# Shorter look-aheads in a pipelined segment mean: indices 7 rows ahead, boundaries closed by three, ids summed 4 ahead

**Chip and metric.** One core of one Trainium2 chip. The metric is device time in microseconds (us) of one execution; medians and ranges are over all executions of a set. A few executions run over 1.5% longer than the fastest of the same kernel; they are called slow, and ratios leave them out. Before: 189.45 us (188.91 to 191.78).

## The reference

```python
n, num_segments = 10_000_000, 10000
data = np.random.randn(n).astype(np.float32)
segment_ids = np.sort(np.random.randint(0, num_segments, n))      # int64, sorted

np.add.at(sums, segment_ids, data)
np.add.at(counts, segment_ids, 1)
return sums / np.maximum(counts, 1)
```

## The kernel before

Each of 128 partitions owns 78,125 numbers, cut into 90 rows of 875. As the ids are sorted and a segment holds some 1,000 numbers, a row has at most about one boundary. Per row the kernel must find where it lies and split the row's sum there. It reads every 175th id (probes), computes from them which window of 175 ids holds the boundary, gathers that window, and sums it; the sum tells the exact place.

The names used below: **first look** (probes to gather indices, six rows at once, VectorE; its last step issues six gathers on GpSimd), **id sum** (`add_ids`, ScalarE), **closing** (`second_look`, VectorE: id sums to boundaries), **total** (ScalarE) and **split** (VectorE) of the row's data. The writer of the kernel fixes every engine's program order: `put(r, steps)` appends steps to what VectorE does after the split of row r, and steps put on one row run in the order in which they were put.

```python
X_PIECE = 15; PIECE = 2; X_DATA = 26; X_LOOK = 9; RING = 18; HALVES = 66
def x_sum(r):
    return 6 if r < HALVES else 5                 # rows by which ids are summed ahead
...
def second_look(a, b):                            # a closing
    ... out=KK[:, a:b], in0=YY[:, a:b], scalar=float(S // K), in1=GS[:, a:b] ...
def total(r):  nc.scalar.activation(out=junk_a, in_=d, func=ACT.Copy, accum_out=T[:, r:r+1])
def split(r):  nc.vector.scalar_tensor_tensor(in0=iota, scalar=KK[:, r:r+1], in1=d,
                   op0=ALU.is_lt, op1=ALU.mult, accum_out=A[:, r:r+1], ...)
...
for a, b in zip(bounds[1:], bounds[2:]):          # groups of six rows, 6, 12, 18, ...
    if a < HALVES:
        put(a - 1, second_look(a, b))
    else:
        put(a - 1, second_look(a, a + 3))
        put(a + 2, second_look(a + 3, b))
for g in range(HEAD, NG):                         # HEAD = 3
    if g < NG - 1:
        put(max(bounds[g] - X_LOOK, 0), first_look(g), 5)
...
for r in range(-X_PIECE - X_DATA, NR):
    while pnext < NR and pnext <= r + X_PIECE + pnext // bounds[NG - 1] + X_DATA:
        load_probes(...)                          # SyncE, two rows a piece
    while nt < NT and 2 * nt <= r + X_DATA:
        load_data(nt)                             # SyncE, two rows a tile
    while r >= -1 and gs < NR and gs <= r + x_sum(gs):
        add_ids(gs)
    if r >= 0:
        total(r); split(r)
        for f in after[r]: f()
```

(Shortened: counters, the first pieces and the steps before row 0 are left out.)

Of the kernel before, what the change touches and what calls it, by code (L numbers as in the profile page):

```python
# [22 lines left out]
NR = 90  # L23
# [4 lines left out]
NX = NR + E  # L28
FAR = float(1 << 18)
GROUPS = [6] * 15  # L30
X_PIECE = 15
PIECE = 2
X_DATA = 26
X_LOOK = 9
RING = 18
HALVES = 66
NO = 79
SHIFT = 6
ND = 2 * SHIFT + 1
# [79 lines left out]
def kernel(  # L119
# [21 lines left out]

    ctx.enter_context(tc.manual_schedule())

    def x_sum(r):
        return 6 if r < HALVES else 5


    pr = cpool.tile([P, NR + 1, K], I64, name="pr")
# [7 lines left out]
    bounds = [0]  # L156
# [3 lines left out]
    def load_probes(r0, r1):  # L160
        a = 0 if r0 == 0 else K * r0 + 1
        b = min(K * r1 + 1, NPR)
        nc.sync.dma_start(out=pr_flat[:, a:b], in_=ids_p[:, a * S : (b - 1) * S + 1 : S])
# [3 lines left out]
    def load_data(t):  # L167
        d = dpool.tile([P, 2 * L], FP32, name="data_t")
        a, b = 2 * t * L, min(2 * (t + 1) * L, D)
        c = b if t < NT - 1 else a + L  # L170
        nc.sync.dma_start(out=d[:, 0 : c - a], in_=data_p[:, a:c])
        if c < b:
            nc.sync.dma_start(out=d[:, c - a : b - a], in_=data_p[:, c:b])
        tiles[t] = d
# [9 lines left out]
    def view(ap, dims):  # L184
        return bass.AP(ap.tensor, ap.offset, [list(ap.ap[0])] + dims)
# [71 lines left out]
    def first_look(g):  # L257

        a, b = bounds[g], bounds[g + 1]
        n = b - a  # L260
        far = fpool.tile([P, n], FP32, name="far", bufs=3)
        last = b == NR
        v = nc.vector

        def s1():
            if last:
                m = NR * K + 1 - NPR
                v.tensor_copy(
                    out=pr_flat.bitcast(I32)[:, 2 * NPR : 2 * (NPR + m)].rearrange("p (a b) -> p a b", b=2),
                    in_=view(snt32[:, 0:1], [[0, m], [1, 2]]),  # L270
                )
            v.tensor_reduce(out=SG[:, a:b], in_=pr32[:, a:b, 0 : 2 * K : 2], axis=AX.X, op=ALU.add)  # L272

        def s2():
            v.scalar_tensor_tensor(  # L275
                out=ST[:, a:b], in0=VI[:, a + 1 : b + 1], scalar=float(K), in1=SG[:, a:b],
                op0=ALU.mult, op1=ALU.subtract,
            )

        def s3():  # L280
            v.tensor_scalar(out=far, in0=ST[:, a:b], scalar1=0.0, scalar2=FAR, op0=ALU.is_equal, op1=ALU.mult)  # L281

        def s4():
            v.tensor_add(out=ST[:, a:b], in0=ST[:, a:b], in1=far)  # L284

        def s5():
            for c, d, w in [(a, b - 1, S), (b - 1, b, TAIL)] if last else [(a, b, S)]:
                v.scalar_tensor_tensor(  # L288
                    out=IDX[:, c:d], in0=ST[:, c:d], scalar=float(w), in1=wb[:, c:d], op0=ALU.mult, op1=ALU.add
                )  # L290
            v.scalar_tensor_tensor(  # L291
                out=YY[:, a:b], in0=ST[:, a:b], scalar=float(K + 1), in1=SG[:, a:b], op0=ALU.mult, op1=ALU.add
            )
            if last:
                v.tensor_scalar(
                    out=tl, in0=ST[:, NR - 1 : NR], scalar1=-1.0, scalar2=float(TAIL - S),
                    op0=ALU.add, op1=ALU.mult,
                )
            gather(g)

        return [s1, s2, s3, s4, s5]

    def gather(g):
        for r in range(bounds[g], bounds[g + 1]):
            nc.gpsimd.indirect_dma_start(  # L305
                out=GT[:, r % RING, :],
                out_offset=None,
                in_=ids2d[:],
                in_offset=bass.IndirectOffsetOnAxis(ap=IDX[:, r : r + 1], axis=0),
                bounds_check=N - W,  # L310
                oob_is_err=False,
            )

    def add_ids(r):
        nc.scalar.activation(  # L315
            out=junk_a[:, 0:W], in_=gt32[:, r % RING, 0 : 2 * W : 2], func=ACT.Copy,
            accum_out=GS[:, r : r + 1],
        )

    def second_look(a, b):  # L320
        def s1():
            nc.vector.scalar_tensor_tensor(  # L322
                out=KK[:, a:b], in0=YY[:, a:b], scalar=float(S // K), in1=GS[:, a:b],
                op0=ALU.mult, op1=ALU.subtract,
            )
            if b == NR:
                nc.vector.tensor_add(out=KK[:, NR - 1 : NR], in0=KK[:, NR - 1 : NR], in1=tl)

        return [s1]

    def total(r):
        n = min(L, D - r * L)
        d = tiles[r // 2][:, (r % 2) * L : (r % 2) * L + n]
        t = T[:, r : r + 1]
        nc.scalar.activation(out=junk_a[:, 0:n], in_=d, func=ACT.Copy, accum_out=t)  # L335
# [152 lines left out]
    def check_frame():  # L488

        return [  # L490
            lambda: v.tensor_sub(out=jb[:, 0:1], in0=base1, in1=pin),
            lambda: v.scalar_tensor_tensor(
                out=bad[:, NC + 1 : NC + 2], in0=base1, scalar=float(NT1), in1=vx, op0=ALU.add, op1=ALU.is_gt
            ),
            lambda: v.tensor_sub(out=jb[:, 1:2], in0=V[:, R2 : R2 + 1], in1=V[:, NR : NR + 1]),
            lambda: v.tensor_scalar(
                out=bad[:, NC + 2 : NC + 3], in0=delta, scalar1=0.0, scalar2=None, op0=ALU.is_lt
            ),
            lambda: v.scalar_tensor_tensor(
                out=bad[:, NC : NC + 1], in0=pc, scalar=0.0, in1=jb[:, 0:1], op0=ALU.is_equal, op1=ALU.mult  # L500
            ),
            lambda: v.tensor_scalar(
                out=bad[:, NC + 3 : NC + 4], in0=delta, scalar1=float(ND - 1), scalar2=None, op0=ALU.is_gt
            ),
            lambda: v.scalar_tensor_tensor(
                out=bad[:, NC + 4 : NC + 5], in0=jb[:, 1:2], scalar=plast[:, 0:1], in1=pone,
                op0=ALU.add, op1=ALU.is_lt,
            ),
        ]
# [159 lines left out]
    def place(c0, c1, t, outs):  # L669
        def s1():  # L670
            n = c1 - c0
            nc.vector.tensor_tensor(
                out=shf[:, c0:c1, 0:ND], in0=view(t[:, c0 : c0 + 1], [[1, n], [1, ND]]),
                in1=view(dm[:, 0:1], [[0, n], [1, ND]]), op=ALU.mult,
            )

        def s2():
            for a, b, d, o in outs:
                nc.vector.tensor_reduce(out=o, in_=shf[:, a:b, 0:d], axis=AX.X, op=ALU.add)

        return [s1, s2]
# [86 lines left out]
    NG = len(GROUPS)  # L768
# [8 lines left out]
    def put(r, steps, every=1):  # L777
        for i, f in enumerate(steps):
            after[r + i // every].append(f)
# [4 lines left out]
    for a, b in zip(bounds[1:], bounds[2:]):  # L784
        if a < HALVES:
            put(a - 1, second_look(a, b))
# [2 lines left out]
            put(a + 2, second_look(a + 3, b))  # L789
    for g in range(HEAD, NG):  # L790
        if g < NG - 1:
            put(max(bounds[g] - X_LOOK, 0), first_look(g), 5)

    def mixed(p, q):
        out = []
# [22 lines left out]
    put(59, counts(Q1, R1), 2)  # L818
    put(R1 - 1, mixed(sums(Q1, R1), select(H1, M1)) + table(H1, M1, tab), 2)
    put(64, place(0, T1, tab, [(0, C1, ND + 1, OUT[:, 0:C1]), (C1, T1, ND + 1, xa[:, 0 : T1 - C1, RM - R1])]))  # L820
    look = bounds[NG - 1] - X_LOOK - 2
    put(46, check_frame(), 2)
    put(66, check_windows())
    put(68, pick(nc.vector, pa[:, :, 0 : RM - R1], C1, CA - C1, R1, RM))
# [23 lines left out]
    pnext = 0  # L848
    nt = 0
    gs = 0  # L850
    for r in range(-X_PIECE - X_DATA, NR):
        while pnext < NR and pnext <= r + X_PIECE + pnext // bounds[NG - 1] + X_DATA:
            n = GROUPS[0] if pnext == 0 else PIECE
            load_probes(pnext, pnext + n)
            if pnext == 0:
                load_data(0)
                nt = 1
            pnext += n
        while nt < NT and 2 * nt <= r + X_DATA:
            load_data(nt)  # L860
            nt += 1
        if r == -X_DATA:
            nc.scalar.dma_start(
                out=snt[0 : P - 1, :],
                in_=segment_ids[D : N].rearrange("(p d) -> p d", d=D)[:, 0:1],
            )
        if r == -1:
            for f in after[r][: 5 * HEAD]:
                f()
        while r >= -1 and gs < NR and gs <= r + x_sum(gs):  # L870
            add_ids(gs)
            gs += 1
        if r == -1:
            for f in after[r][5 * HEAD :]:
                f()
        if r >= 0:
            total(r)
            split(r)
            for f in after[r]:
                f()  # L880
# [31 lines left out]
```

## Time and profile before

| | before |
|---|---|
| median | 189.45 us |
| span of the profiled run | 186.4 us |
| VectorE (DVE) busy | 140.8 us, 76% |
| ScalarE (ACT) busy | 136.6 us, 73% |
| 90 gathers | 14.0 MB, 23.5% of the DMA engines' span |
| data and probes | 40.5 MB, 73.8% |

No engine is busy all the time; only the DMA is, from 5 to 172 us. The lines that carry this stand in the prediction.

### The profile page before, as it was taken

To read this page: it belongs to the slowest core of one execution; us is meant where nothing else is said; L and a number is where in the kernel's file an instruction comes from. 1 tells how busy PE (TensorE), PEld (TensorE's weight loads), DVE (VectorE), ACT (ScalarE), POOL (GpSimd) and SP (SyncE) were. 2 spreads that over 40 slices of the span, in tenths; PEclk is the share of its full clock that TensorE was granted. 3 is DMA by queue.
4 is the path that set the end of the run, shared out by engine and by line. 5 is a ranking of instruction groups with operands and counts; after the bars stand their busy time and mean duration, and the time that the engine had idled before them with its cause. 6 is when DMAs were issued, how large, how long until landed. Compare 5 with 4: busy or idle time off the path is not lost.

```text
span 186.4 us, 1479 instructions
## 1 busy us (share of the span) xinstructions
PE 1.6 (1%) x6; PEld 1.4 (1%) x6; DVE 140.8 (76%) x438; ACT 136.6 (73%) x362; POOL 99.9 (54%) x119
## 2 busy tenths in 40 slices
PE   0000000000002000000000000000000000010000
PEld 0000000000001000000000000000000000010000
DVE  6321397979197796858879997686899989999881
ACT  8010599967999497895959949599886786989940
POOL 5687775076734828266471664727347287883000
DMA  6999999999999999999999999999998999999000
GB/s 28 178 178 340 331 325 328 306 341 330 316 330 319 338 333 305 326 335 332 314 310 335 318 328 317 329 344 307 326 246 246 343 405 406 405 406 391 15 0 12
DMA packets 70613, 54.63 MB, mean 293 GB/s; under 512 B 60464, under 2 KB 61032, under 8 KB 70599
## 3 DMA queue, kind: packets, MB, share of 16 engines
q1 hardware_dynamic: 64667, 40.50, 73.8%
q0 software_dynamic: 5760, 14.01, 23.5%
q14 instruction: 14, 0.11, 0.2%
q10 hardware_dynamic: 172, 0.00, 0.1%
HBM read 56.59 MB, written 0.04 MB: 304 GB/s over the span
## 4 chain that ended last, share of the span: by engine, by line
DMA 33%; issue 32%; ACT 14%; POOL 13%; DVE 4%; POOLq 1%; ACTq 0%
DMA GT<-in_segment_ids_dram,IDX 23%; POOL GT L305 12%; DMA data_t<-in_data_dram 10%; ACT junk_a L335 9%; ACT junk_a L315 5%; POOLq L305 1%; DVE jj L236 0%; POOL i_i L198 0%; DVE junk_v L340 0%; DVE most L745 0%; DVE add L737 0%; POOL pb L703 0%; DVE sel L648 0%; DVE most L751 0%; POOL KL L689 0%
## 5 line engine op out<-in xcount | busy, mean ns | idle before, releaser
L305 POOL DMA_INDIRECT GT<-in_segment_ids_dram,IDX x90 | 90.9, 1010 | 66.9 <-ACT junk_a L315 33.5
L340 DVE SCALAR_TENSOR_TENSOR junk_v<-iota,q,data_t 128x875 bf16<-128x875 f32 x90 | 100.6, 1118 | 8.0 <-DMA data_t<-in_data_dram 6.7
L335 ACT ACTIVATE junk_a<-data_t 128x875 bf16<-128x875 f32 x90 | 83.6, 929 | 3.7 <-DMA data_t<-in_data_dram 0.7
L315 ACT ACTIVATE junk_a<-GT 128x175 bf16<-128x175 int32 x90 | 32.4, 360 | 38.1 <-DMA GT<-in_segment_ids_dram,IDX 35.9
L322 DVE SCALAR_TENSOR_TENSOR q<-YY,GS 128x6 f32<-128x6 f32 (+1 forms) x19 | 3.3, 171 | 21.7 <-ACT junk_a L315 21.7
L315 ACT ACTIVATION_READ_ACCUMULATOR junk_a<-GT 128x1 f32 x90 | 16.8, 187 | 0.0
L335 ACT ACTIVATION_READ_ACCUMULATOR junk_a<-data_t 128x1 f32 x90 | 16.8, 186 | 0.0
L340 DVE DVE_READ_ACCUMULATOR junk_v<-iota,q,data_t 128x1 f32 x90 | 7.4, 83 | 0.0
L272 DVE TENSOR_REDUCE SG<-pr 128x6 f32<-128x30 int32 x15 | 2.7, 180 | 5.7 <-DMA snt<-in_segment_ids_dram 3.3
L281 DVE TENSOR_SCALAR far<-ST 128x6 f32<-128x6 f32 x15 | 2.7, 178 | 0.5
L187 ACT ACTIVATE GT<-q 128x3150 int32<-128x3150 f32 x1 | 3.0, 2996 | 0.0
L284 DVE TENSOR_TENSOR ST<-ST,far 128x6 f32<-128x6 f32 x15 | 2.6, 170 | 0.5
L288 DVE SCALAR_TENSOR_TENSOR IDX<-ST,wb 128x6 int32<-128x6 f32 (+2 forms) x16 | 2.6, 165 | 0.5
L275 DVE SCALAR_TENSOR_TENSOR ST<-pr,SG 128x6 f32<-128x6 int32 x15 | 2.5, 166 | 0.5
L291 DVE SCALAR_TENSOR_TENSOR YY<-ST,SG 128x6 f32<-128x6 f32 x15 | 2.4, 161 | 0.0
L187 ACT ACT_TABLE_LOAD x1 | 1.3, 1283 | 0.7 <-PEq L896 0.7
L584 DVE TENSOR_TENSOR q<-T,q 128x44 f32<-128x44 f32 (+3 forms) x4 | 0.7, 178 | 1.4 <-ACT junk_a L335 1.4
L704 POOL TENSOR_SCALAR pb<-pb 128x168 f32<-128x168 f32 (+1 forms) x2 | 1.6, 784 | 0.2
L544 PE MATMUL badp<-bads,ones 128*128 128x1 f32 x2 | 0.6, 362 | 104.7 <-DVE bads L543 104.7
L236 DVE CAST jj<-jj_i 128x128 f32<-128x128 int32 x1 | 0.8, 840 | 0.7 <-POOL jj_i L235 0.7
L571 DVE RECIPROCAL ct<-ct 128x16 f32<-128x16 f32 (+2 forms) x4 | 1.2, 300 | 0.1
L544 PEld LDWEIGHTS badp<-bads,ones 128*128 128x128 f32 x2 | 0.5, 310 | 104.8 <-DVE bads L543 104.8
(129 smaller groups left out, 45.2 us busy)
## 6 DMA issues: line engine op xcount, KB each, us to landing
data_t<-in_data_dram SPq DMA_DIRECT2D x44, 875.0 KB, 10.6
GT<-in_segment_ids_dram,IDX POOLq DMA_INDIRECT x90, 6.4
pr<-in_segment_ids_dram SPq DMA_DIRECT2D x41, 10.0 KB, 8.1
data_t<-in_data_dram SPq DMA_DIRECT2D x1, 437.5 KB, 18.6
data_t<-in_data_dram SPq DMA_DIRECT2D x1, 125.0 KB, 15.8
out_dram<-OUT SPq DMA_DIRECT2D x1, 36.6 KB
pr<-in_segment_ids_dram SPq DMA_DIRECT2D x1, 31.0 KB, 4.0
snt<-in_segment_ids_dram ACTq DMA_DIRECT2D x1, 1.0 KB
```

Of the source, the lines that this page charges most:

```text
L187: nc.scalar.activation(out=gt32[:, :, 0 : 2 * W : 2], in_=view(q5[:, 0, 0:1], [[0, RING], [0, W]]), func=ACT.Copy)
L272: v.tensor_reduce(out=SG[:, a:b], in_=pr32[:, a:b, 0 : 2 * K : 2], axis=AX.X, op=ALU.add)
L275: v.scalar_tensor_tensor(out=ST[:, a:b], in0=VI[:, a + 1 : b + 1], scalar=float(K), in1=SG[:, a:b], op0=ALU.mult, op1=ALU.subtract,)
L281: v.tensor_scalar(out=far, in0=ST[:, a:b], scalar1=0.0, scalar2=FAR, op0=ALU.is_equal, op1=ALU.mult)
L284: v.tensor_add(out=ST[:, a:b], in0=ST[:, a:b], in1=far)
L288: v.scalar_tensor_tensor(out=IDX[:, c:d], in0=ST[:, c:d], scalar=float(w), in1=wb[:, c:d], op0=ALU.mult, op1=ALU.add)
L291: v.scalar_tensor_tensor(out=YY[:, a:b], in0=ST[:, a:b], scalar=float(K + 1), in1=SG[:, a:b], op0=ALU.mult, op1=ALU.add)
L305: nc.gpsimd.indirect_dma_start(out=GT[:, r % RING, :], out_offset=None, in_=ids2d[:], in_offset=bass.IndirectOffsetOnAxis(ap=IDX[:, r : r ...
L315: nc.scalar.activation(out=junk_a[:, 0:W], in_=gt32[:, r % RING, 0 : 2 * W : 2], func=ACT.Copy, accum_out=GS[:, r : r + 1],)
L322: nc.vector.scalar_tensor_tensor(out=KK[:, a:b], in0=YY[:, a:b], scalar=float(S // K), in1=GS[:, a:b], op0=ALU.mult, op1=ALU.subtract,)
L335: nc.scalar.activation(out=junk_a[:, 0:n], in_=d, func=ACT.Copy, accum_out=t)
L340: nc.vector.scalar_tensor_tensor(out=junk_v[:, 0:n], in0=iota[:, 0:n], scalar=KK[:, r : r + 1], in1=d, op0=ALU.is_lt, op1=ALU.mult, accum_ ...
```

## The change

The intent: less look-ahead for gathers and probes, so that less stands in the DMA queues ahead of the data, and finer closings so that VectorE does not wait for six id sums at once.

```diff
-X_PIECE = 15
+X_PIECE = 6
+LATE = 66
-X_LOOK = 9
+X_LOOK = 7
-HALVES = 66
+HALVES = 18
+    def lead(r):
+        return X_LOOK if r < LATE else 9 if r < bounds[NG - 1] else 11
     def x_sum(r):
-        return 6 if r < HALVES else 5
+        return 6 if r < HALVES else 4 if r < LATE else 5
@@
-            put(max(bounds[g] - X_LOOK, 0), first_look(g), 5)
+            put(bounds[g] - lead(bounds[g]), first_look(g), 5)
@@
-        while pnext < NR and pnext <= r + X_PIECE + pnext // bounds[NG - 1] + X_DATA:
+        while pnext < NR and pnext <= r + lead(pnext) + X_PIECE + X_DATA:
```

(Cut: the start of the loop over r, and the variable `look`, which keeps its value.)

> **What bounds the kernel now.** The kernel walks 90 rows of 875 numbers per partition. Each row needs three transfers: its data (448 KB, the SyncE queue), probes of the sorted ids (1,280 single ids for two rows, the same queue) and one gathered window of 175 ids per partition (GpSimd's queue). ScalarE sums the ids of a later row (L315) and the row's data (L335); VectorE closes boundaries (L322), splits the row (L340) and, between rows, makes the gather indices of a later group of six (L272 to L291) and builds the output.
>
> I read the strip of busy tenths first, then a table of stretches, then waits, then VectorE and ScalarE row by row in the timeline.
>
> ```profile
> DVE  6321397979197796858879997686899989999881
> ACT  8010599967999497895959949599886786989940
> DMA  6999999999999999999999999999998999999000
> GB/s 28 178 178 340 331 325 328 306 341 330 316 330 319 338 333 305 326 335 332 314 310 335 318 328 317 329 344 307 326 246 246 343 405 406 405 406 391 15 0 12
> ```
>
> The DMA engines are full from about 5 us to 172 us of the 186.4 us span; nothing else is. They move some 325 GB/s while probes and gathers run among the data, and 405 at the end.
>
> ```profile
> 60.00:80.00 20.00, 0.00 (x0) 0.00 (x0) 14.77 (x51) 14.98 (x43) 10.18 (x12) 1.00 1.09 328
> 136.00:140.00 4.00, 0.00 (x0) 0.00 (x0) 3.79 (x13) 3.17 (x10) 2.11 (x2) 1.00 0.98 227
> 140.00:144.00 4.00, 0.00 (x0) 0.00 (x0) 4.00 (x11) 2.81 (x8) 3.09 (x4) 1.00 0.83 260
> 152.00:156.00 4.00, 0.00 (x0) 0.00 (x0) 3.53 (x15) 2.25 (x7) 3.09 (x4) 1.00 1.00 403
> 172.00:186.40 14.40, 0.00 (x0) 0.00 (x0) 9.07 (x35) 6.91 (x16) 0.00 (x0) 1.00 0.06 18
> ```
>
> (Columns: stretch, length, busy PE, PE loads, VectorE, ScalarE, GpSimd, clock, DMA share, GB/s.) The share is about 1.08 in mid kernel[...], and drops below 1 only at 136 to 144 us: there SyncE had issued two probe pieces in a row (133.28 to 137.39 us in the timeline) and data ran short.
>
> ```profile
> ACT junk_a L315 <- DMA GT<-in_segment_ids_dram,IDX: 35.9, 24, 6.4
> DVE q L322 <- ACT junk_a L315: 21.7, 10, 6.9
> DVE junk_v L340 <- DMA data_t<-in_data_dram: 6.7, 12, 0.8
> ```
>
> These three waits look like the prize: ScalarE waits for gathers, VectorE for ScalarE's id sums, and only a little for data. But 15 or so of the 35.9 us and 6.9 of the 21.7 us fall in the start, before row 0. In the rest VectorE's waits alternate: ids at a group's start, then data in that same group.
>
> ```profile
> 72.47 0.17 DVE L322 SCALAR_TENSOR_TENSOR q<-YY,GS 128x6 f32<-128x6 f32 x1 [1.83 <-ACT junk_a L315]
> 75.87 1.13 DVE L340 SCALAR_TENSOR_TENSOR junk_v<-iota,q,data_t 128x875 bf16<-128x875 f32 x1 [0.60 <-DMA data_t<-in_data_dram]
> ...
> 128.76 0.17 DVE L322 SCALAR_TENSOR_TENSOR q<-YY,GS 128x6 f32<-128x6 f32 x1 [1.36 <-ACT junk_a L315]
> 129.86 1.13 DVE L340 SCALAR_TENSOR_TENSOR junk_v<-iota,q,data_t 128x875 bf16<-128x875 f32 x1 [0.33 <-DMA data_t<-in_data_dram]
> 133.03 0.18 DVE L584 TENSOR_TENSOR q<-T,q 128x18 f32<-128x18 f32 x1 [0.60 <-ACT junk_a L335]
> 144.62 1.13 DVE L340 SCALAR_TENSOR_TENSOR junk_v<-iota,q,data_t 128x875 bf16<-128x875 f32 x1 [0.51 <-DMA data_t<-in_data_dram]
> 152.30 1.13 DVE L340 SCALAR_TENSOR_TENSOR junk_v<-iota,q,data_t 128x875 bf16<-128x875 f32 x1 [0.83 <-DMA data_t<-in_data_dram]
> 177.57 0.17 DVE L584 TENSOR_TENSOR q<-T,q 128x10 f32<-128x10 f32 x1 [0.80 <-ACT junk_a L335]
> ```
>
> Counting splits, 61.26 us is row 24 and 152.30 us row 72, both just as their data land: 91.0 us for 48 rows, 1.90 us each. That is the DMA's pace (448 + 179 + 5 KB at 325 to 330 GB/s is 1.93 us). After row 72 VectorE waits once more, 0.80 us, and otherwise works through to 182.3 us. So the end is: landing of rows 72 and 73, plus 30.0 us of nearly solid VectorE work. A wait removed earlier pays only if those rows land earlier.
>
> **What the Trainium skill says.** "DMA: Bandwidth & Descriptors", section "Queues, rings and completion order": an engine goes round robin over its queues packet by packet, each queue in ring order. The trace fits: gathers land in 6.4 us (median) beside a data queue that needs 10.6. So order among probes and data is what SyncE issues; gathers cut in. The same page, "Why small descriptors are slow": a fixed overhead per packet. Here 60,464 packets are under 512 B; taking 98.8 us for 40.0 MB of data at 405 GB/s out of queue 1's 137.6 us (73.8%) leaves an estimated 38.8 us for probes, 0.43 us per row. "Perfetto Trace Analysis", section "DMA Instruction — HWDGE (DVE, Sync)": the time shown for an issue is waiting for and using the descriptor generator, not moving data. SyncE's data issues take 0.33 us at least and 2.6 us in the median, so I read the excess as back pressure from full DMA engines.
>
> **The change, part by part.** The built programs differ thus.
>
> (1) Gather indices for groups starting at rows 18 to 60 are made two rows later (7 ahead, not 9); from row 66 on (9) and for the last group (11) as before. Ids are summed 4 rows ahead, not 6. So ScalarE meets a gather three rows after its indices, as before; the gather wait is not lengthened in rows. A gather costs the DMA 43.8 us / 90 = 0.49 us per row (23.5% of the span).
>
> (2) Probes run 13 rows ahead of data instead of 15 below row 66: five pieces before the second data tile instead of six; one more back-to-back pair of pieces where row 66's piece is issued, beside data tile 25. From there SyncE's order is identical.
>
> (1) and (2) together let data land earlier by 2 x (0.43 + 0.49) / 1.08 = 1.7 us up to about row 50. It is a loan: between rows 50 and 66 the distances grow back, and the DMA has moved the same bytes by row 66. Rows 72 and 73 gain nothing.
>
> (3) Boundaries are closed three rows at a time from row 18. VectorE then needs ids up to row a+2, not a+5, before row a, and the second three only three rows later, when they were summed one ScalarE row earlier than needed. This removes most of the 12.4 us of ids waits after row 18 (3.97, 0.81, 1.83, 1.27, 0.98, 2.21, 1.36). At L322's cost it adds eight instructions of about 0.17 us, 1.4 us in all, only one of them after 128.76 us and that overlapped to about 0.1 us. Of the removed time nearly all turns into waiting for data: by 144.62 us VectorE is gated by row 68 whatever it saved.
>
> What is left on the path: the 0.80 us wait at 177.57 us may go if ScalarE runs earlier, since its last hard waits (2.20 us at 145.21, 1.69 at 155.07 in its timeline) hang on index making at VectorE rows 63 and 69: -0.5. The gate at row 72 may shift a little, as fewer gathers sit in the queue just before: -0.5. The extra pair of probe pieces: the pair at 133 us cost (1.08-0.98) x 4 + (1.08-0.83) x 4 = 1.4 us of DMA time; half of it, as gathers may fill the hole here: +0.5 to +0.7. Extra L322: +0.1. Sum -0.3 us. Taking 188.9 as the base (188.91, 189.5 and the profiled run's 188.19; 191.78 looks like an outlier) gives about 188.5.
>
> **Rivals.** (A) Compute-bound: the loop of index making, gather, id sum, boundary sets the pace, and the data waits are its echo. For: over 12 rows the loop measures 15.1 us (ids of row 29 summed at 60.14 to those of 36 at 75.26) plus 7.7 us of six id sums, 1.9 us per row, the same as DMA. One VectorE row and half a group's ids come off. If DMA had room, five groups of 1 to 2 us would give 181 to 184. Against: DMA share never sags in mid kernel, and bytes ahead of the last rows are unchanged. (B) The loan is partly kept: VectorE, 1.7 us early at row 42, does its housekeeping of rows 42 to 53 (no wait at all from 94.61 to 117.74 us) early and stays early into the last stage: 186 to 187.5. Against: rows 68 and 72 still gate. (C) Thinner lead: gathers come too late, or two probe pairs starve data twice: 190 to 192. For: the hole at 140 us is real. Against: ScalarE has 2 us of slack per group.
>
> **Range and chances.** My account gives 188.5; (B) pulls to 186, (C) to 191. Executions of one kernel spread by about 1 us. I take 185.9 to 190.7. A gain over 2% means below 185.7, which needs (A): 0.12. A loss over 2% means above 193.3, which needs (C) at its worst: 0.04. Within 2%: 0.84.
>
> **What would show it.** Right: waits of L322 for L315 after row 18 fall from about 12 us to under 4 while L340's waits for data rise from 6.7 to 10 or more; row 36 splits about 1.7 us earlier than 83.69; row 72 splits at 152.3 within 1 us; DMA share still about 1.08, with a dent near 100 us. Wrong: row 72 splits 3 us or more earlier, or DMA ends well before 172 us (then A or B); or ScalarE's gather waits grow beyond 36 us (C).

## The result

| | median, us | lowest to highest | ratio to before |
|---|---|---|---|
| before | 189.45 | 188.91 to 191.78 | |
| changed | 196.84 | 195.81 to 197.58 | 1.038 [1.031, 1.044] |

Ratios here and below are the mean time of one kernel's fast runs over that of the other's of the same rounds, with a 95% interval, so not quite the ratio of the medians. The change is 3.8% slower: outside the stated range, and in the class that was given 0.04.

The changed kernel's page, strip of busy tenths (span 195.8 us):

```profile
DVE  6322677787293893929849998494669999989991
DMA  6899999999999999999999999999999999950000
GB/s 27 169 252 322 321 339 337 317 326 305 332 326 322 319 342 323 308 331 309 314 273 260 279 340 330 303 338 328 250 356 382 408 398 408 394 150 11 0 0 12
```

The data are in at nearly the same time as before (the DMA share falls from 1.02 in the microsecond from 171 us to 0.46 in the next; before, from 0.97 to 0.58), but from 172 us on 24 us follow instead of 14, and GpSimd issues its last gather at 174.93 us instead of 164.8. VectorE shows a regular hole, a low digit every second or third slice. So the data no longer set the end. The waits of the changed kernel (L319 is the id sum, L326 the closing, L588 uses row totals, L339 makes them):

```profile
ACT junk_a L319 <- DMA GT<-in_segment_ids_dram,IDX: 39.6, 21, 4.8
DVE q L326 <- ACT junk_a L319: 32.4, 10, 4.3
DVE q L588 <- ACT junk_a L339: 3.8, 2, 2.9
```

VectorE's wait for id sums rose from 21.7 to 32.4 us where it should have fallen, and the line of splits that wait for data (6.7 us before) is gone altogether. ScalarE's waits for gathers rose too, from 35.9 us to 39.6, or to 46.1 with its first wait, of 6.5 us, which this page puts down to VectorE (L285) and the page of before to a gather. The timeline shows where VectorE's waits sit; one round, of VectorE's closings and GpSimd's gathers among ScalarE's sums:

```profile
64.47 0.16 DVE L326 SCALAR_TENSOR_TENSOR q<-YY,GS 128x3 f32<-128x3 f32 x1 [3.75 <-ACT junk_a L319]
64.58 0.18 DVE L276 TENSOR_REDUCE SG<-pr 128x6 f32<-128x30 int32 x1
...
76.30 0.16 DVE L326 SCALAR_TENSOR_TENSOR q<-YY,GS 128x3 f32<-128x3 f32 x1 [3.28 <-ACT junk_a L319]
76.40 0.18 DVE L276 TENSOR_REDUCE SG<-pr 128x6 f32<-128x30 int32 x1
...
78.16 1.00 POOL L309 DMA_INDIRECT GT<-in_segment_ids_dram,IDX  x1 [4.31 <-ACT junk_a L319]
...
83.89 0.36 ACT L319 ACTIVATE junk_a<-GT 128x175 bf16<-128x175 int32 x1 [1.95 <-DMA GT<-in_segment_ids_dram,IDX]
...
88.25 0.16 DVE L326 SCALAR_TENSOR_TENSOR q<-YY,GS 128x3 f32<-128x3 f32 x1 [3.60 <-ACT junk_a L319]
```

Read it as a circle. At 76.30 the closing of rows 30 to 32 gets its id sums. Right behind it in VectorE's program stands the first look of group 36 (L276 is its first step); it needs nothing from that closing, but could not start earlier, because the closing in front had been waiting for 3.28 us. Its indices let the first gather go at 78.16 (the line names an id sum of ScalarE as what ended GpSimd's wait, but in all seven rounds below the first gather starts 0.69 to 0.70 us after the first look's last step, whatever is named); that gather lands and row 36's ids are summed at 83.89; two more id sums (one of them waits for its own gather, and totals stand between) release the next closing at 88.25, and with it the first look of group 42. One round is 11.95 us. From the closing at 52.27 us to that at 137.49 us there are seven rounds: 12.17 us each, for six rows. (One closing of them, at 112.23 us, did not wait; VectorE's own work came last there.)

Why the change did this: group g is looked at in row `bounds[g] - 7`, which is `a - 1` of the group before. That is the row on which that group's closing is put, and closings are put first. At 9 ahead it was row `a - 3`, with no closing in front.

By VectorE's split starts, the changed kernel is behind the kernel before by 1.9 us at row 18, 4.5 at row 24, 8.3 at row 60, 10.7 at row 66 and 9.4 at row 89. Rows 24 to 60 take 12.07 us per six rows instead of 11.43; rows 18 to 24 already take one round, 12.36 us, where they took 9.82 before; rows 60 to 66 lose 2.3 us more at L588 (2.93 us waited against 0.60), as ScalarE's totals are late too.

### The profile page after: what moved, and what is told of

It is laid out like the page before. It is cut to its first block, busy times and chain, and to the rows that moved or that the text cites. A ratio compares the mean times of both kernels' runs of the same rounds, so it can differ in the third digit from the quotient of the medians.

```text
span 195.8 us, 1488 instructions
## 1 busy us (share of the span) xinstructions
PE 1.6 (1%) x6; PEld 1.4 (1%) x6; DVE 140.9 (72%) x446; ACT 136.6 (70%) x362; POOL 99.7 (51%) x119
## 4 chain that ended last, share of the span: by engine, by line
SPq 29%; DMA 27%; issue 23%; ACT 15%; POOL 3%; DVE 2%; POOLq 0%; ACTq 0%
SPq L175 22%; DMA GT<-in_segment_ids_dram,IDX 20%; ACT junk_a L339 8%; ACT junk_a L319 7%; DMA data_t<-in_data_dram 6%; SPq L167 6%; POOL GT L309 3%; DMA pr<-in_segment_ids_dram 0%; DVE most L749 0%; DVE add L741 0%; DVE most L755 0%; DVE junk_v L344 0%; DVE OUT L758 0%; DVE most L758 0%; DVE wp L726 0%
## 5 line engine op out<-in xcount | busy, mean ns | idle before, releaser
L339 ACT ACTIVATE junk_a<-data_t 128x875 bf16<-128x875 f32 x90 | 83.6, 929 | 2.8
L319 ACT ACTIVATE junk_a<-GT 128x175 bf16<-128x175 int32 x90 | 32.4, 360 | 48.4 <-DMA GT<-in_segment_ids_dram,IDX 39.6
L326 DVE SCALAR_TENSOR_TENSOR q<-YY,GS 128x3 f32<-128x3 f32 (+1 forms) x27 | 4.4, 163 | 32.6 <-ACT junk_a L319 32.4
L319 ACT ACTIVATION_READ_ACCUMULATOR junk_a<-GT 128x1 f32 x90 | 16.8, 187 | 0.0
L339 ACT ACTIVATION_READ_ACCUMULATOR junk_a<-data_t 128x1 f32 x90 | 16.8, 186 | 0.0
L276 DVE TENSOR_REDUCE SG<-pr 128x6 f32<-128x30 int32 x15 | 2.7, 183 | 8.6 <-DMA pr<-in_segment_ids_dram 8.5
L588 DVE TENSOR_TENSOR q<-T,q 128x44 f32<-128x44 f32 (+3 forms) x4 | 0.7, 180 | 3.9 <-ACT junk_a L339 3.8
L285 DVE TENSOR_SCALAR far<-ST 128x6 f32<-128x6 f32 x15 | 2.8, 188 | 0.5
```

The source lines that it names most:

```text
L276: v.tensor_reduce(out=SG[:, a:b], in_=pr32[:, a:b, 0 : 2 * K : 2], axis=AX.X, op=ALU.add)
L285: v.tensor_scalar(out=far, in0=ST[:, a:b], scalar1=0.0, scalar2=FAR, op0=ALU.is_equal, op1=ALU.mult)
L319: nc.scalar.activation(out=junk_a[:, 0:W], in_=gt32[:, r % RING, 0 : 2 * W : 2], func=ACT.Copy, accum_out=GS[:, r : r + 1],)
L326: nc.vector.scalar_tensor_tensor(out=KK[:, a:b], in0=YY[:, a:b], scalar=float(S // K), in1=GS[:, a:b], op0=ALU.mult, op1=ALU.subtract,)
L339: nc.scalar.activation(out=junk_a[:, 0:n], in_=d, func=ACT.Copy, accum_out=t)
```

## The experiments

Theory **Q** (queue): the first look stands behind a closing on VectorE, which makes a circle of 12 us. Rivals: **S** (id sums only 4 rows ahead are too late), **P** (the probes 13 rows ahead, and the extra pair of pieces, starve the data), **T** (indices 7 rows ahead are too late, in whatever order). The times were taken in rounds with the kernel before on the same chip (before: 188.95 to 189.5 us in the four sets). Results were correct except where said; the record holds no refused run and no run e6. e5_look7 was executed once, so it has no ratio and its state (fast or slow) is unknown.

| run | what it is | median, us | ratio |
|---|---|---|---|
| e1_swap | changed; first look ahead of closing | 189.88 | 1.001 [0.993, 1.009] |
| e2_look8 | changed; first look 8 ahead | 189.03 | 0.998 [0.991, 1.006] |
| e3_ids6 | changed; ids 6 ahead | 202.72 | 1.071 [1.064, 1.077] |
| e4_probes | before; probes 13 ahead | 189.80 | 1.001 [0.994, 1.007] |
| e5_look7 | before; first look 7 ahead | 227.93 | one execution |
| e7_halves_ids4 | before; closings by three, ids 4 ahead | 189.96 | 1.001 [0.992, 1.011] |
| e8_ones | changed; closings row by row (wrong result) | 189.80 | 1.003 [0.995, 1.011] |
| e9_swap_probes15 | e1_swap; probes as before | 188.83 | 0.998 [0.992, 1.004] |
| e10_look7_first | e5_look7; first look ahead of closing | 195.82 | 1.036 [1.030, 1.043] |
| e11_ones_mended | e8_ones mended | 189.60 | 0.999 [0.990, 1.007] |
| e12_late84 | e1_swap; LATE = 84 | 191.46 | 1.017 [1.008, 1.027] |
| e13_look8_probes15 | e2_look8; probes as before | 191.21 | 1.009 [1.003, 1.014] |

Five of these sets hold one slow execution each; without it their medians are 189.84 (e1), 188.51 (e2), 189.22 (e7), 189.29 (e11) and 191.45 us (e12).

**e1_swap: exchange the two.** The loop that puts first looks is moved in front of the loop that puts closings. The same instructions run, with two neighbours exchanged once per group:

```diff
+    for g in range(HEAD, NG):
+        if g < NG - 1:
+            put(bounds[g] - lead(bounds[g]), first_look(g), 5)
     for a, b in zip(bounds[1:], bounds[2:]):
...
-    for g in range(HEAD, NG):
-        if g < NG - 1:
-            put(bounds[g] - lead(bounds[g]), first_look(g), 5)
```

> The changed kernel, with the gather indices of the next group put ahead of the closing that falls on the same row (row a-1). Theory Q (the indices of group a+6 are queued on VectorE behind the closing of a to a+2, which waits for id sums; one round of that loop is about 9.0 us from an id sum to the next gather's landing plus 3.1 us of two more id sums, 12.1 us per six rows): the loop opens, L344 waits for data again, 187 to 190 us, and VectorE's waits at closings fall from 32 us to under 20. Rival S (ids summed 4 rows ahead are too late): 196 to 197, unchanged. Rival P (probes 13 rows ahead, and the extra pair of pieces, starve the data): unchanged. Rival T (indices 7 rows ahead are too late in whatever order): 194 or more.

189.88 us: the whole loss is gone, as Q said and the three rivals did not. VectorE's timeline in e1_swap, at the closing of rows 24 to 26:

```profile
58.54 0.18 DVE L276 TENSOR_REDUCE SG<-pr 128x6 f32<-128x30 int32 x1
...
59.36 0.17 DVE L292 SCALAR_TENSOR_TENSOR IDX<-ST,wb 128x6 int32<-128x6 f32 x1
59.45 0.16 DVE L295 SCALAR_TENSOR_TENSOR YY<-ST,SG 128x6 f32<-128x6 f32 x1
59.73 0.16 DVE L326 SCALAR_TENSOR_TENSOR q<-YY,GS 128x3 f32<-128x3 f32 x1
```

The indices are ready at 59.5 us, before the closing, which now waits for next to nothing. The waits of e1_swap:

```profile
DVE junk_v L344 <- DMA data_t<-in_data_dram: 11.2, 11, 2.1
DVE q L326 <- ACT junk_a L319: 4.9, 3, 2.3
DVE q L326 <- issue: 3.4, 2, 3.1
DVE q L326 <- ACT junk_a L339: 2.1, 2, 1.1
```

Waits at closings fell from 32.4 to 10.4 us (4.9, 3.4 and 2.1; under 20 was expected), and the data are what VectorE waits for again. Row 72 splits as its data land:

```profile
154.09 1.13 DVE L344 SCALAR_TENSOR_TENSOR junk_v<-iota,q,data_t 128x875 bf16<-128x875 f32 x1 [0.89 <-DMA data_t<-in_data_dram]
```

**e2_look8: one row earlier.** Indices on row a-2, probes left as in the changed kernel.

```diff
+    def look_at(r):
+        return 8 if r < LATE else lead(r)
-            put(bounds[g] - lead(bounds[g]), first_look(g), 5)
+            put(bounds[g] - look_at(bounds[g]), first_look(g), 5)
```

> The changed kernel with the gather indices 8 rows ahead instead of 7 below row 66, so that they fall on row a-2, which has no closing in front of them; probes, three-row closings and ids 4 ahead as in the changed kernel. Theory Q: one row is enough to leave the queue behind the closing, so the loop opens: 187.5 to 190.5 us, waits at closings under 15 us. Rival T (lateness in rows is what costs, some 3.7 us per row moved): 192 to 194.

189.03 us. One row is worth all of it. T's price per row does not hold.

**e3_ids6: sum the ids earlier.**

```diff
-        return 6 if r < HALVES else 4 if r < LATE else 5
+        return 6 if r < LATE else 5
```

> The changed kernel with ids summed 6 rows ahead again below row 66, all else kept. Theory Q: the round of the loop does not hold the distance of the sums at all, so 195 to 198. Rival S: back to 188 to 191. P and T: unchanged, 196 to 197.

202.72 us. S is out: earlier sums make it worse. But Q's own range was missed by 5 us. Its circle is there unchanged (rows 24 to 60 take 11.96 us per six), and what came on top is another wait. VectorE's waits in e3_ids6:

```profile
DVE q L326 <- ACT junk_a L319: 22.8, 7, 4.7
DVE q L588 <- ACT junk_a L339: 7.8, 4, 5.0
DVE q L414 <- ACT junk_a L339: 5.6, 1, 5.6
```

L414 and L588 use row totals, made by ScalarE. With ids six ahead, an id sum that waits for its gather stands in front of two more totals in ScalarE's program; VectorE waits 13.4 us for totals against 3.8 in the changed kernel. It is the same kind of fault on the other engine, and it suggests why 4 ahead went with 7 ahead.

**e4_probes: the probes alone,** on the kernel before.

```diff
-        while pnext < NR and pnext <= r + X_PIECE + pnext // bounds[NG - 1] + X_DATA:
+        while pnext < NR and pnext <= r + (13 if pnext < 66 else X_PIECE) + pnext // bounds[NG - 1] + X_DATA:
```

> The kernel before with only the probes moved: 13 rows ahead of the data below row 66, 15 above. Theory Q, S and T: 188.5 to 190.5, with a dent of the DMA share near 100 us that costs under 1 us. Rival P: 193 or more.

189.80 us, as if nothing had been done. P is out.

**e5_look7: the later look alone,** on the kernel before, with closings by six.

```diff
-            put(max(bounds[g] - X_LOOK, 0), first_look(g), 5)
+            put(bounds[g] - (7 if bounds[g] < 66 else X_LOOK), first_look(g), 5)
```

> The kernel before with only the gather indices moved, 7 rows ahead of groups 18 to 60 instead of 9; closings by six and ids 6 ahead stay. Theory Q: now the indices are queued behind a closing of all six rows, so one round is 9.0 us plus five further id sums of 1.54 us, 16.7 us per group against 11.2 now; eight groups, 8 x 5.5 = 44 us more: 225 to 237 us, with ScalarE waiting some 7 us for each group's first gather. Rival T (two rows later is what costs): 196 to 200. S and P: 189, as ids and probes are as before.

227.93 us in its one execution, where Q had 225 to 237. The arithmetic holds in the single round as well; from e5_look7's timeline (L322 is its closing):

```profile
74.80 0.17 DVE L322 SCALAR_TENSOR_TENSOR q<-YY,GS 128x6 f32<-128x6 f32 x1 [2.51 <-ACT junk_a L315]
74.91 0.18 DVE L272 TENSOR_REDUCE SG<-pr 128x6 f32<-128x30 int32 x1
...
82.56 0.36 ACT L315 ACTIVATE junk_a<-GT 128x175 bf16<-128x175 int32 x1 [6.74 <-DMA GT<-in_segment_ids_dram,IDX]
...
91.16 0.17 DVE L322 SCALAR_TENSOR_TENSOR q<-YY,GS 128x6 f32<-128x6 f32 x1 [7.89 <-ACT junk_a L315]
```

From closing to closing 16.4 us (16.7 expected): 7.8 us to the next group's first id sum, then 8.6 us until its sixth is there. So the later look does the harm without the change's other parts; closing by three cut it down to what was measured.

**e7_halves_ids4: the other two parts alone,** on the kernel before.

```diff
-        return 6 if r < HALVES else 5
+        return 6 if r < 18 else 4 if r < HALVES else 5
-        if a < HALVES:
+        if a < 18:
```

> The kernel before with closings by three from row 18 and ids 4 ahead below row 66; indices 9 ahead and probes 15 ahead as before. Theory Q: these two parts do no harm alone: 187.5 to 190.5, L340 waits more for data and L322 less for id sums, as the prediction had it. Rival S (4 ahead is too late): 194 or more.

189.96 us. Waits of e7_halves_ids4:

```profile
DVE junk_v L340 <- DMA data_t<-in_data_dram: 20.1, 20, 2.2
DVE q L322 <- ACT junk_a L315: 9.6, 3, 6.5
```

This is what the prediction had told of the whole change: waits for ids (21.7 us before) become waits for data (6.7 us before), about one for one, and the time stays.

**e8_ones and e11_ones_mended: closings row by row.** The first look stays behind a closing, but that closing needs one id sum.

```diff
-            put(a - 1, second_look(a, a + 3))
-            put(a + 2, second_look(a + 3, b))
+            for c in range(a, b, 1 if a < LATE else 3):
+                put(c - 1, second_look(c, c + (1 if a < LATE else 3)))
```

> The changed kernel with boundaries of rows 18 to 65 closed one row at a time; the indices still stand behind the closing on row a-1, but that closing now waits for the ids of row a alone. Theory Q: a round is 9.0 us with no further id sums, under the 9.2 us that ScalarE needs for six rows anyway: 188 to 191.5 us though VectorE has 32 instructions more. S, T and P: 196 or more, as none of what they blame is touched.

189.80 us, but a wrong result: two counting passes on rows 41 and 59 read boundaries that this edit closes only later in the program. e11_ones_mended moves those passes (41 to 43, 59 to 60):

> e8_ones with the two counting passes that read the closed boundaries moved behind the last one they read (row 43 instead of 41, row 60 instead of 59). A correct result, and the time of e8_ones within 1 us: 188.5 to 191.

189.60 us and correct. Three rounds of the same queue, with six, three and one id sums behind the gather, cost 228, 197 and 189.6 us: the round, not the queue as such, decides, and it stops mattering once it is shorter than the data's pace (9.0 us by Q's estimate in the last, against 11.4). The last two differ in the closings and in the two moved passes alone. The first differs from them in ids (6 ahead) and probes as well; with ids 6 ahead closing by three took 202.72 us (e3_ids6).

**e9_swap_probes15: e1_swap with the probes of before.**

```diff
-        while pnext < NR and pnext <= r + lead(pnext) + X_PIECE + X_DATA:
+        while pnext < NR and pnext <= r + (17 if pnext >= bounds[NG - 1] else 15) + X_DATA:
```

> e1_swap with the probes 15 rows ahead as in the kernel before (SyncE's order is that of before). Theory Q with the data as the limit: 188 to 190, the same as e1_swap within 1 us; the second dent of the DMA share near 100 us goes away. If the extra pair of probe pieces costs what its dent shows, this is 0.5 to 1.5 us faster than e1_swap.

188.83 us, ratio 0.998. If the extra pair of probe pieces costs anything it is under what these intervals resolve.

**e10_look7_first: e5_look7 with the first look put ahead of the closing** (the move of e1_swap).

> The kernel before with the indices 7 rows ahead of groups 18 to 60 and placed ahead of the closing on the same row; closings by six, ids 6 ahead, probes 15 ahead. It is e5_look7 with two neighbouring pieces of VectorE's program exchanged. Theory Q: the one-group round of 16.9 us is gone; what is left is a round over two groups, last id sum of a group, closing, six rows of about 1.35 us, indices and gather 9.0 us, then six id sums, about 25 us per 12 rows or 12.5 per six, 1.3 more than before over eight groups: 196 to 203 us. Rival T (lateness itself): the same 228 as e5_look7.

195.82 us, just under the range; rows 24 to 60 take 12.40 us per six, against 12.5 worked out. The exchange of neighbours is worth 32 us here. What is left is for T: with closings by six, a look 7 ahead is late in any order. The round over two groups that Q worked out is seen in the waits at closings, which are long in every other group (6.61, 0.90, 5.80, 1.07, 5.41 us from row 18 on). With closings by three (e1_swap) that round is short enough.

**e12_late84 and e13_look8_probes15: attempts to beat both.** e12_late84 is e1_swap with `LATE = 84`; e13_look8_probes15 joins the edits of e2_look8 and e9_swap_probes15.

> An attempt to beat both: e1_swap with the 7-row indices, 13-row probes and ids 4 ahead kept up to row 84 instead of 66, so that less stands in the DMA queues ahead of the data of row 72. Two rows of probes and gathers fewer ahead are about 1.7 us; against it three probe pieces now follow each other before row 84's. If the DMA's order is what sets the end: 187 to 189. If the three pieces starve the data: 189 to 191.

191.46 us, slower by 1.7% (the 2% verdict is unclear). Row 72 did split earliest of all, at 151.78 us; it did not wait for data itself, row 70 had (1.34 us). Its last 17 rows then took 31.9 us instead of 29 to 30. Three probe pieces in a row were followed by a hole in the bytes (128 GB/s at a DMA share of 0.98); a window of e12_late84:

```profile
140.00:144.00 4.00, 0.00 (x0) 0.00 (x0) 4.00 (x10) 3.30 (x11) 2.72 (x3) 1.00 0.98 128
```

After 150 us ScalarE waits 3.8 us for gathers and VectorE 1.9 at closings and 1.7 for totals. That the hole caused those waits is not shown: e7_halves_ids4 moved only 103 GB/s in the same window, after two pieces in a row, and lost nothing.

> The best candidate of the earlier runs: indices 8 rows ahead (e2_look8) with the probes in SyncE's order of the kernel before (e9_swap_probes15), closings by three, ids 4 ahead below row 66. Theory Q with the data as the common floor: no better than the kernel before, ratio 0.99 to 1.00 (187.5 to 189.5 us), since rows 72 and after still wait for the same bytes. A ratio of 0.98 or less would say that the floor is not the data.

191.21 us, 0.9% slower than before and not the 0.99 to 1.00 expected. Its data came late (row 72 at 155.62 us; the DMA share from 140 to 160 us was 0.97, 1.03 in e9_swap_probes15), with SyncE's order that of the kernel before. But e7_halves_ids4 had a share of 0.97 there too, and two of the six executions of e13_look8_probes15 took 189.62 and 189.86 us. Why two harmless edits add up to this stays open. No version beat the kernel before beyond the noise.

## Why the prediction was wrong

**What bounds the kernel before: right, as far as tested.** Six correct versions in which the circle is open or short (e1, e2, e4, e7, e9, e11), which differ in every part of the change, lie within 0.2% of the kernel before (the intervals reach up to 1% to either side). Their waits for data grew to 11 to 20 us, and in each of them row 72 split at 152.6 to 155.3 us just as its data landed, with 29 to 30 us to the last split. So the data look like a floor under all of them; no run moved fewer bytes to show it. (Rival A, the circle of the kernel before as the limit, predicted a gain from opening it; none came.)

**The step that failed** is in parts (1) and (3) of the sum. Part (1) said "So ScalarE meets a gather three rows after its indices, as before; the gather wait is not lengthened in rows", and part (3) said of closing by three that "This removes most of the 12.4 us of ids waits after row 18". Both counted distances in rows. They did not ask what stands in front of the first look in VectorE's program. Two rows later is the row of a closing, and behind it. The term "nearly all turns into waiting for data" should have been a circle of its own: measured, 1.9 us from closing to gather, 5.7 to the id sum of the gathered row, 4.4 to the third sum, 11.95 us a round against a data pace of about 11.4. The ids waits after row 18 were 24.7 us (4.27, 3.75, 3.28, 3.60, 3.44, 3.16, 3.15), not under 4. The prediction says how "the built programs differ", but in distances and counts; it does not look at the order on one row.

**Chances.** Rival C (slower, 190 to 192, from gathers that come too late) named the right direction and half the cause: gathers did come late, and its sign, ScalarE's gather waits beyond 36 us, came (39.6 or 46.1). But it laid this to a thinner lead, made the loss too small, and was dismissed because "ScalarE has 2 us of slack per group". That slack was real, but it is spent once per group by a circle that lengthens by more.

**Part (2) and the loan: right in kind.** The probes alone are free (e4). In e1_swap rows 32 and 34, which wait for data in both kernels, split 1.4 and 1.7 us earlier than before (1.7 foretold), row 38 at the same time and row 56 1.6 us later, gated so too. By these two executions the loan came, and was paid back sooner than foretold. In the changed kernel nothing of it is left: row 36 split at 89.34 us, where 1.7 us before 83.69 was foretold. One term was mis-sized: the page moves 14.0 MB in 90 gathers, 156 KB each and not 179, so the DMA's pace works out at 1.86 us a row instead of 1.93 (1.90 measured); nothing hangs on it. The dent near 100 us came (DMA share 0.91 from 100 to 104 us in the changed kernel) and cost nothing there, as the data were ahead.

**The Trainium skill.** "Perfetto Trace Analysis", section "DVE / Act Engine Instruction (TENSOR_ADD, Activation, etc)", names an event-wait FIFO between sequencer and engine. The prediction cited three sections on the DMA and not this one, which bears on the change most. The traces agree with a strict queue: after each of the waiting closings above the first look starts 0.10 to 0.11 us after the closing's start, never during its wait, though none of these first looks shows a wait of its own for probes.

## What to carry to other kernels

When work on an in-order engine is moved, list what now stands in front of it, and ask of each of those instructions what it waits for; a distance in rows says nothing of that. If what is moved feeds, through a transfer, the very thing that is waited for, write down the circle and its time per round, and compare it with the present pace. Put the producer of a long latency ahead of a wait, never behind it: here that is two neighbouring pieces exchanged, for 7 us (32 us with closings by six).

## What the Trainium skill lacked or had wrong

- "Perfetto Trace Analysis", the section above: it names the FIFO and draws nothing from it for the order of a program. That the queue keeps its order is not lacking in the skill; what a waiting instruction in front of an independent one costs was not found in it. Here: 227.93 against 195.82 us, and 196.84 against 189.88, for the same instructions in another order.
- "DMA: Bandwidth & Descriptors", section "Anatomy of one DMA — SWDGE (gpsimd) path": fixed 2.0 us plus bytes over 436 GB/s would give an estimated 2.4 us for a gather (14.0 MB over 90 is 156 KB). In the kernel before gathers landed after 6.4 us in the median, and after 5.4 to 7.2 us between 20 and 130 us, beside a full data queue. For a circle through a gather the loaded figure is the one that counts.
